# The matmuls of the w_out and down products, regrouped by stationary operand across two PSUM banks

## The chip, the cores and the metric

The kernel runs on one core of a Trainium2 chip. The metric is the device time of one execution in microseconds (us), measured from outside the profile; lower is better. A profiled execution also has a span, which runs from its first to its last recorded instruction and is a little shorter than its device time.

The engines have short names in the profile. PE is TensorE running matmuls, and PEld is TensorE loading a stationary operand. DVE is VectorE, ACT is ScalarE, POOL is GpSimd. SP is the engine that issues most of the transfers.

## The reference

The kernel computes one layer of an encoder on 512 tokens of width 1024, all in float32:

```python
n = rms_norm(h, norm_mix_pre)
proj = n @ w_in                       # gMLP u, v | q, k, v | gates
y_a = gmlp_spatial_gating(gelu(z_gmlp), ...)
y_b = mixture of three dilated window attentions
merged = g_a * (y_a @ w_branch_a) + g_b * (y_b @ w_branch_b)
mix_out = merged @ w_out
h = h + rms_norm(mix_out, norm_mix_post)
n2 = rms_norm(h, norm_mlp_pre)
hid = square(relu(n2 @ w_up))
mlp_out = hid @ w_down
h = h + rms_norm(mlp_out, norm_mlp_post)
```

The change touches two of these products: `merged @ w_out`, in which 1024 values are summed for each output, and `hid @ w_down`, in which 4096 are.

## The kernel before

**A product in three parts.** Each float32 operand is split into a high part and a low part in a reduced format, fp32r: ACT writes `hi`, and DVE writes `lo = raw - hi`. A product of two operands is then three matmuls into one PSUM bank: `mm3` (lines 82 to 86) issues high by high (L84), high by low (L85) and low by high (L86). In the first two the stationary operand, the one held in the array, is the same tile `ah`; in the third it is `al`.

**The two products of the change.** Both are token-major: tokens are the rows of the output. There are four token tiles `t` of 128 tokens, and each has two output halves `hf` of 512 columns. Each half has a PSUM bank of its own, so `all_banks` (line 526) takes all eight banks: `accs[t][hf]`. The stationary operand is the activation (`mh`, `ml` for w_out; `hh`, `hl` for down), a block of 128 features by the 128 tokens of `t`. The moving operand is 512 columns of the weight. So the two halves of one token tile use the same stationary operands.

w_out has 8 blocks `k` of 128 features, down has 32 blocks `f`. For the first 4 blocks of w_out, and the first 28 of down, the order is block by block, and within a block `t`, `hf`, and the three parts. The last four blocks (`KLAST`, `NLAST`) are kept in SBUF and run token tile by token tile: for each `t`, the whole of half 0 (4 blocks by 3 parts, 12 matmuls), then the whole of half 1. So a tile's outputs are finished one after the other while the matmuls of later tiles still run. w_out has 192 matmuls and down 768.

**What follows a token tile.** `post_norm` (line 529) takes a tile's two banks. For each half, ACT squares it and sums the squares (L534), and DVE multiplies it by the gain (`y`, L538). With the second half, DVE finishes the sum of squares (L90 and L93) and POOL raises it to the power -0.5 (L96). DVE then scales and adds the residual (L541, two instructions). After down, the result goes out in two transfers (L659). After w_out there is a second norm (L574 squares, `xn` L578), eight transposes on PE (`pt`, L581), and the split into `n2h` and `n2l` (L79, L80), which the up product reads.

**From w_out to up.** The up product (`pu`) starts with the first two token tiles only: for its first four blocks it does columns 0 to 255 first, and columns 256 to 511 once all four are begun. These short matmuls fill PE while the norms of the last token tiles finish.

**What sets the order.** Each engine runs its instructions in order. The framework places the instructions of each engine by a timeline that it simulates when the kernel is built, so an instruction may stand on its engine at another place than the code has it; the transposes of a token tile stand some microseconds after its norm, among other matmuls.

Of the kernel before, what the change touches and what calls it, by code (L numbers as in the profile page):

```python
# [19 lines left out]
KD = D // P  # L20
FF = 4096
KF = FF // P
# [14 lines left out]
def block_kernel(ctx: ExitStack, tc: tile.TileContext, x, norm_mix_pre, w_in, b_gate, ln_v_gain, ln_v_bias,  # L37
                 w_spatial, b_spatial, w_branch_a, w_branch_b, w_out, norm_mix_post, norm_mlp_pre, w_up,
                 w_down, norm_mlp_post, ident_c, rope_c, mask_c, perm_c, out):
    nc = tc.nc  # L40
# [22 lines left out]
    def wload(shape, srcs, name):  # L63
        raw = wpool.tile([P] + shape, F32, name=name, tag="raw")
        for dst, src in srcs(raw):
            nc.sync.dma_start(dst, src)
        return raw

    def wsplit(raw, pl=None, bufs=None, tag="w", sub=None):
        pl = pl or wpool  # L70
        shape = list(raw.shape)
        hi = pl.tile(shape, F32R, name="hi", tag=tag + "hi", bufs=bufs)
        lo = pl.tile(shape, F32R, name="lo", tag=tag + "lo", bufs=bufs)
        nc.scalar.activation(hi, raw, AF.Copy)  # L74
        (sub or nc.vector).tensor_tensor(lo, raw, hi.bitcast(F32), op=ALU.subtract)  # L75
        return hi, lo

    def split_into(hi, lo, src):
        nc.scalar.activation(hi, src, AF.Copy)  # L79
        nc.vector.tensor_tensor(lo, src, hi.bitcast(F32), op=ALU.subtract)  # L80

    def mm3(ps, a, b, start, stop):
        (ah, al), (bh, bl) = a, b
        nc.tensor.matmul(ps, ah, bh, start=start, stop=False)  # L84
        nc.tensor.matmul(ps, ah, bl, start=False, stop=False)  # L85
        nc.tensor.matmul(ps, al, bh, start=False, stop=stop)  # L86

    def rstd_of(ss, mult, eps=EPS):
        t = small.tile([P, 1], F32, name="rs_in")
        nc.vector.tensor_scalar(t, ss[:, 0:1], mult, eps, op0=ALU.mult, op1=ALU.add)  # L90
        if ss.shape[1] == 2:
            t2 = small.tile([P, 1], F32, name="rs_in2")
            nc.vector.scalar_tensor_tensor(t2, ss[:, 1:2], mult, t, op0=ALU.mult, op1=ALU.add)  # L93
            t = t2
        r = small.tile([P, 1], F32, name="rs_out")
        nc.gpsimd.tensor_tensor(r, t, neghalf[:, :1], op=ALU.pow)  # L96
        return r
# [16 lines left out]
    start = ExitStack()  # L114
# [63 lines left out]
    for i in range(4):  # L178
        if i + 1 < 4:
            norm_x(blocks[i + 1], xts[i + 1])  # L180
        b = blocks[i]
        pv = psA.tile([P, GW], F32, name="pv", tag="acc", bufs=4)
        for k in range(KD):
            sl = slice(b * P, (b + 1) * P)
            mm3(pv, (nh[:, k, sl], nl[:, k, sl]), w0[k], k == 0, k == KD - 1)
        split_into(v0h[:, b], v0l[:, b], pv)
# [32 lines left out]
    def feature_tile(wh, wl, nk, mh, ml, tag="acc"):  # L219
        ps = psA.tile([P, S], F32, name="pf", tag=tag, bufs={"acc": 4, "S": 2}[tag])  # L220
        for k in range(nk):
            mm3(ps, (wh[:, k], wl[:, k]), (mh[:, k], ml[:, k]), k == 0, k == nk - 1)
        return ps
# [237 lines left out]
    for g2 in range(2):  # L461
        raw = wload([KD, 2 * P], lambda r: [(r, fcols(w_in, COL_U + g2 * 2 * P, KD, 2 * P))], "uw")
        for j in range(2):
            g = 2 * g2 + j
            wh, wl = wsplit(raw[:, :, j * P:(j + 1) * P], sub=nc.gpsimd)
            ps = feature_tile(wh, wl, KD, nhn, nln, "S")
# [5 lines left out]
            t = gpool.tile([P, 4, P], F32, name="sv", bufs=2)  # L472
# [10 lines left out]
    mh = mpool.tile([P, KD, S], F32R, name="mh")  # L483
    ml = mpool.tile([P, KD, S], F32R, name="ml")
    gp = ExitStack()
    gapool = pool(gp, "gapool", bufs=2)
    for d2 in range(4):
# [3 lines left out]
        for j in range(2):  # L491
# [3 lines left out]
            for br in range(2):  # L495
                wh, wl = wsplit(raws[br][:, :, sl])
                ps = feature_tile(wh, wl, KD, nhn, nln)
# [26 lines left out]
    halves = [slice(0, 512), slice(512, 1024)]  # L524

    def all_banks():
        return [[psB.tile([P, 512], F32, name="pd", tag=tg, bufs=4) for _ in range(2)] for tg in ("tp", "tp", "acc", "acc")]

    def post_norm(pss, gain, yp, dst, res):
        ss = small.tile([P, 2], F32, name="ss2")  # L530
        ys = []
        for hf, hs in enumerate(halves):
            junk = yp.tile([P, 512], F32, name="junk", bufs=1)
            nc.scalar.activation(junk, pss[hf], AF.Square, accum_out=ss[:, hf:hf + 1])  # L534
            if hf:
                r = rstd_of(ss, 1.0 / D)
            y = yp.tile([P, 512], F32, name="y", bufs=2)
            nc.vector.tensor_tensor(y, pss[hf], gain[:, hs], op=ALU.mult)  # L538
            ys.append(y)
        for hf, hs in enumerate(halves):  # L540
            nc.vector.scalar_tensor_tensor(dst[:, hs], ys[hf], r, res[:, hs], op0=ALU.mult, op1=ALU.add)  # L541
# [3 lines left out]
    wopool = pool(wo, "wopool", bufs=KLAST)  # L545
    accs = all_banks()

    def w_out_mm(t, k, hf, wh, wl):
        ts_ = slice(t * P, (t + 1) * P)
        mm3(accs[t][hf], (mh[:, k, ts_], ml[:, k, ts_]), (wh[:, halves[hf]], wl[:, halves[hf]]), k == 0, k == KD - 1)  # L550

    last = []
    for k0 in range(0, KD, 2):
        raw = wload([2, D], lambda r: [(r, w_out[k0 * P:(k0 + 2) * P].rearrange("(k p) c -> p k c", p=P))], "wow")
        for j in range(2):
            k = k0 + j
            if k < KD - KLAST:
                wh, wl = wsplit(raw[:, j])
                for t in range(4):
                    for hf in range(2):  # L560
                        w_out_mm(t, k, hf, wh, wl)
            else:
                last.append((k, *wsplit(raw[:, j], wopool, tag="wo")))
    ypool = pool(wo, "ypool")
    for t in range(4):
        ts_ = slice(t * P, (t + 1) * P)
        for hf in range(2):
            for k, wh, wl in last:
                w_out_mm(t, k, hf, wh, wl)
        post_norm(accs[t], gain2[:, 0], ypool, h2[:, t], h2[:, t])  # L570
        ss = small.tile([P, 2], F32, name="ss")
        for hf, hs in enumerate(halves):
            junk = ypool.tile([P, 512], F32, name="junk", bufs=1)
            nc.scalar.activation(junk, h2[:, t, hs], AF.Square, accum_out=ss[:, hf:hf + 1])  # L574
        r = rstd_of(ss, 1.0 / D)
        xn = ypool.tile([P, D], F32, name="xn2")
        for q, hs in enumerate(halves):
            nc.vector.scalar_tensor_tensor(xn[:, hs], h2[:, t, hs], r, gain2[:, 1, hs], op0=ALU.mult, op1=ALU.mult)  # L578
            pt = psB.tile([P, 4, P], F32, name="pt2", tag="tp", bufs=4)
            for j in range(4):  # L580
                nc.tensor.transpose(pt[:, j], xn[:, (4 * q + j) * P:(4 * q + j + 1) * P], ident)  # L581
            ks = slice(4 * q, 4 * q + 4)
            split_into(n2h[:, ks, ts_], n2l[:, ks, ts_], pt)
# [24 lines left out]
    for f2 in range(KF // 2):  # L608
        raw = wload([KD, 2 * P], lambda r: [(r, fcols(w_up, f2 * 2 * P, KD, 2 * P))], "upw")
        for j in range(2):  # L610
            f = 2 * f2 + j
            wh, wl = wsplit(raw[:, :, j * P:(j + 1) * P], *((epool, None, "e") if f < NSPLIT - 3 else ()))
            ps = psB.tile([P, S], F32, name="pu", tag="acc", bufs=4)
# [14 lines left out]
    lpool = pool(dn, "lpool", bufs=NLAST)  # L628
    accs = all_banks()

    def down(t, f, hf, hh, hl, wh, wl):
        ts_ = slice(t * P, (t + 1) * P)
        mm3(accs[t][hf], (hh[:, ts_], hl[:, ts_]), (wh[:, halves[hf]], wl[:, halves[hf]]), f == 0, f == KF - 1)

    last = []
    for f2 in range(KF // 2):
        raw = wload([2, D], lambda r: [(r, w_down[f2 * 2 * P:(f2 + 1) * 2 * P].rearrange("(k p) c -> p k c", p=P))], "dnw")
        for j in range(2):
            f = 2 * f2 + j
            end = f >= KF - NLAST  # L640
            wh, wl = wsplit(raw[:, j], *((lpool, 1, "l") if f == KF - NLAST else ()))
            hp = lpool if end else dpool
            hh = hp.tile([P, S], F32R, name="hh")
            hl = hp.tile([P, S], F32R, name="hl")
            split_into(hh, hl, hids[f])
            if end:
                last.append((f, hh, hl, wh, wl))
            else:
                for t in range(4):
                    for hf in range(2):  # L650
                        down(t, f, hf, hh, hl, wh, wl)
    for t in range(4):
        for hf in range(2):
            for f, hh, hl, wh, wl in last:
                down(t, f, hf, hh, hl, wh, wl)
        o = lpool.tile([P, D], F32, name="o", bufs=2)
        post_norm(accs[t], gain2[:, 2], lpool, o, h2[:, t])
        for hs in halves:
            nc.sync.dma_start(out[t * P:(t + 1) * P, hs], o[:, hs])  # L659
# [41 lines left out]
```

## Time and profile before

| | |
|---|---|
| Time, median of 3 runs | 842.24 us (841.08 to 842.56) |
| The profiled execution | 842.03 us, of which its span is 840.2 us |
| PE busy in the span | 826.9 us, 98% |
| Instructions | 9719, of which 3867 matmuls and 3867 loads of a stationary operand |
| w_out's matmuls | from 436.0 to 481.1 us |
| down's matmuls | from 659.8 to 833.7 us |

Matmuls overlap: the profile gives each one a duration of 389 ns, but the next one starts before it ends. What a stream of matmuls costs is read from the distance between their starts. A matmul's row has the line of `mm3` that issued it, its output `pd` and its two operands; the profile sorts the operands by name, so `pd<-hi,hh` is the high part of the weight against the high part of the hidden activation.

### The profile page before, as it was taken

How to read it: one execution, taken by the hardware profiler on the slowest of the kernel's cores; microseconds unless marked ns; L12 is line 12 of the kernel's file. 1: busy time of each engine (PE TensorE's matmuls, PEld its weight loads, DVE VectorE, ACT ScalarE, POOL GpSimd, SP SyncE). 2: the span in 40 equal slices, each digit the busy share in tenths (PEclk: the TensorE clock that was granted, in tenths of full speed). 3: DMA queues.
4: the chain of work that ended last, by engine and by line, in shares of the span. 5: the costliest groups of instructions: out<-in, count | busy, mean ns of one | idle time of the engine just before them, and what ended most of it. 6: DMA issues, size and time to landing. Idle time of an engine off the chain costs nothing. (4 is left out here: it accounts for less than half of the span.)

```text
span 840.2 us, 9719 instructions
## 1 busy us (share of the span) xinstructions
PE 826.9 (98%) x3867; PEld 693.9 (83%) x3867; DVE 419.4 (50%) x711; ACT 293.3 (35%) x479; POOL 74.9 (9%) x67
## 2 busy tenths in 40 slices
PE   7999999999999999999999999999999999999997
PEld 5899888888888778888888898888888888888885
DVE  6422788878874647433334744333333433333425
ACT  6322243435344353333233533222222322333312
POOL 2000123232214200000010100000000000000001
PEclk9999999999999999999999999999999999999999
DMA  9433233323114131431457103333323132222202
GB/s 306 129 101 88 68 96 101 84 67 96 56 52 125 51 100 62 140 101 50 151 195 236 44 2 101 100 101 101 101 100 101 53 131 86 87 98 99 101 1 100
DMA packets 69278, 83.14 MB, mean 99 GB/s; under 512 B 1849, under 2 KB 57297, under 8 KB 69234
## 3 DMA queue, kind: packets, MB, share of 16 engines
q1 hardware_dynamic: 67810, 77.67, 29.3%
q0 software_dynamic: 1424, 4.87, 1.7%
q8 instruction: 30, 0.49, 0.2%
q14 instruction: 14, 0.11, 0.0%
HBM read 80.43 MB, written 2.10 MB: 98 GB/s over the span
## 5 line engine op out<-in xcount | busy, mean ns | idle before, releaser
L84 PE MATMUL pf<-nh,hi 128*128 128x512 f32 x352 | 138.7, 394 | 0.6 <-DVE u L445 0.6
L86 PE MATMUL pf<-nh,lo 128*128 128x512 f32 x352 | 139.3, 396 | 0.0
L85 PE MATMUL pf<-nl,hi 128*128 128x512 f32 x352 | 138.1, 392 | 0.0
L85 PE MATMUL pu<-n2l,hi 128*128 128x512 f32 (+1 forms) x288 | 105.9, 369 | 0.1
L84 PE MATMUL pu<-n2h,hi 128*128 128x512 f32 (+1 forms) x288 | 105.1, 368 | 0.0
L86 PE MATMUL pu<-n2h,lo 128*128 128x512 f32 (+1 forms) x288 | 104.5, 364 | 0.0
L85 PE MATMUL pd<-lo,hh 128*128 128x512 f32 x256 | 99.6, 389 | 0.0
L84 PE MATMUL pd<-hi,hh 128*128 128x512 f32 x256 | 99.3, 389 | 0.0
L86 PE MATMUL pd<-hi,hl 128*128 128x512 f32 x256 | 98.6, 389 | 0.0
L75 DVE TENSOR_TENSOR lo<-upw,hi 128x1024 fp32r<-128x1024 f32 x32 | 39.1, 1225 | 103.0 <-ACT hi L74 103.0
L84 PEld LDWEIGHTS pf<-nh,hi 128*128 128x128 f32 x352 | 66.2, 188 | 14.3 <-DVE u L445 0.9
L86 PEld LDWEIGHTS pf<-nh,lo 128*128 128x128 f32 x352 | 66.2, 188 | 14.3 <-issue 0.2
L85 PEld LDWEIGHTS pf<-nl,hi 128*128 128x128 f32 x352 | 66.2, 188 | 14.1
L74 ACT ACTIVATE hi<-upw 128x1024 fp32r<-128x1024 f32 x32 | 33.8, 1060 | 111.7 <-PE pu L85 100.6
L80 DVE TENSOR_TENSOR hl<-hid,hh 128x512 fp32r<-128x512 f32 x32 | 21.9, 691 | 80.6 <-ACT hh L79 80.6
L84 PEld LDWEIGHTS pu<-n2h,hi 128*128 128x128 f32 x288 | 53.8, 188 | 9.9
L86 PEld LDWEIGHTS pu<-n2h,lo 128*128 128x128 f32 x288 | 54.0, 188 | 9.4
L85 PEld LDWEIGHTS pu<-n2l,hi 128*128 128x128 f32 x288 | 54.1, 188 | 8.6 <-DVE n2l L80 0.3
L247 POOL TENSOR_TENSOR sw<-sw,rope 32x512 f32<-32x512 f32 x24 | 42.4, 1767 | 176.8 <-DVE sw L245 159.6
L84 PEld LDWEIGHTS pd<-hi,hh 128*128 128x128 f32 x256 | 48.0, 188 | 10.1
L85 PEld LDWEIGHTS pd<-lo,hh 128*128 128x128 f32 x256 | 48.0, 188 | 10.1
L86 PEld LDWEIGHTS pd<-hi,hl 128*128 128x128 f32 x256 | 48.0, 188 | 9.8
(201 smaller groups left out, 1306.2 us busy)
## 6 DMA issues: line engine op xcount, KB each, us to landing
upw<-in_w_up_dram SPq DMA_DIRECT2D x16, 1024.0 KB, 5.5
dnw<-in_w_down_dram SPq DMA_DIRECT2D x16, 1024.0 KB, 4.8
qkw<-in_w_in_dram SPq DMA_DIRECT2D x24, 512.0 KB, 4.7
gw<-in_w_in_dram SPq DMA_DIRECT2D x8, 1024.0 KB, 5.3
slab<-in_w_in_dram SPq DMA_DIRECT2D x6, 1024.0 KB, 12.8
wow<-in_w_out_dram SPq DMA_DIRECT2D x4, 1024.0 KB, 4.9
w0raw<-in_w_in_dram SPq DMA_DIRECT2D x4, 512.0 KB, 7.0
uw<-in_w_in_dram SPq DMA_DIRECT2D x2, 1024.0 KB, 5.1
```

Of the source, the lines that this page charges most:

```text
L74: nc.scalar.activation(hi, raw, AF.Copy)
L75: (sub or nc.vector).tensor_tensor(lo, raw, hi.bitcast(F32), op=ALU.subtract)
L80: nc.vector.tensor_tensor(lo, src, hi.bitcast(F32), op=ALU.subtract)
L84: nc.tensor.matmul(ps, ah, bh, start=start, stop=False)
L85: nc.tensor.matmul(ps, ah, bl, start=False, stop=False)
L86: nc.tensor.matmul(ps, al, bh, start=False, stop=stop)
L247: nc.gpsimd.tensor_tensor(sw, sw, rope[:, 1], op=ALU.mult)
```

## The change

`mm3_pair` takes both banks of a token tile. It goes through the same three parts, and issues each part for half 0 and then for half 1. So the stationary operand changes twice in six matmuls instead of three or four times, and every matmul writes the other bank of the pair than the one before it. The loops over `hf` go. In the last four blocks of each product the two halves of a token tile now run side by side through the four blocks. Number, shapes and operands of the matmuls stay as they are, and so does everything that follows them.

```diff
+    def mm3_pair(banks, a, bs, start, stop):
+        ah, al = a
+        bhs, bls = zip(*bs)
+        for lhs, rhs, first, last in ((ah, bhs, start, False), (ah, bls, False, False), (al, bhs, False, stop)):
+            for ps, r in zip(banks, rhs):
+                nc.tensor.matmul(ps, lhs, r, start=first, stop=last)
...
-    def w_out_mm(t, k, hf, wh, wl):
+    def w_out_mm(t, k, wh, wl):
         ts_ = slice(t * P, (t + 1) * P)
-        mm3(accs[t][hf], (mh[:, k, ts_], ml[:, k, ts_]), (wh[:, halves[hf]], wl[:, halves[hf]]), k == 0, k == KD - 1)
+        mm3_pair(accs[t], (mh[:, k, ts_], ml[:, k, ts_]), [(wh[:, hs], wl[:, hs]) for hs in halves], k == 0, k == KD - 1)
...
                 for t in range(4):
-                    for hf in range(2):
-                        w_out_mm(t, k, hf, wh, wl)
+                    w_out_mm(t, k, wh, wl)
...
-        for hf in range(2):
-            for k, wh, wl in last:
-                w_out_mm(t, k, hf, wh, wl)
+        for k, wh, wl in last:
+            w_out_mm(t, k, wh, wl)
...
-    def down(t, f, hf, hh, hl, wh, wl):
+    def down(t, f, hh, hl, wh, wl):
         ts_ = slice(t * P, (t + 1) * P)
-        mm3(accs[t][hf], (hh[:, ts_], hl[:, ts_]), (wh[:, halves[hf]], wl[:, halves[hf]]), f == 0, f == KF - 1)
+        mm3_pair(accs[t], (hh[:, ts_], hl[:, ts_]), [(wh[:, hs], wl[:, hs]) for hs in halves], f == 0, f == KF - 1)
...
                 for t in range(4):
-                    for hf in range(2):
-                        down(t, f, hf, hh, hl, wh, wl)
+                    down(t, f, hh, hl, wh, wl)
     for t in range(4):
-        for hf in range(2):
-            for f, hh, hl, wh, wl in last:
-                down(t, f, hf, hh, hl, wh, wl)
+        for f, hh, hl, wh, wl in last:
+            down(t, f, hh, hl, wh, wl)
```

## Rows read from the trace of the kernel before

**Rows 1.** From the profile's page: busy time, share of the span and number of instructions of each engine.

```profile
PE 826.9 (98%) x3867; PEld 693.9 (83%) x3867; DVE 419.4 (50%) x711; ACT 293.3 (35%) x479; POOL 74.9 (9%) x67
```

**Rows 2.** Busy time in three stages: w_out, the start of up, and down. Columns: the stretch in us, its length, busy us (instructions) of each engine, granted clock, share of the transfer engines, GB/s.

```profile
core 0: us, PE busy (x) PEld busy (x) DVE busy (x) ACT busy (x) POOL busy (x), PEclk, DMA share, GB/s
435.90:480.50 44.60, 44.60 (x205) 37.02 (x205) 25.88 (x41) 19.07 (x37) 2.76 (x5) 1.00 0.53 175
480.50:500.00 19.50, 19.42 (x163) 19.10 (x162) 9.81 (x20) 6.47 (x16) 1.65 (x3) 1.00 0.01 2
...
659.00:834.00 175.00, 175.00 (x773) 144.63 (x771) 67.15 (x81) 52.76 (x75) 1.65 (x3) 1.00 0.25 86
```

**Rows 3.** The instructions that write or read the banks `pd`, by line: count, duration in ns (least, median, most), starts of the first and the last in us. The rows with `hh` and `hl` are down's, those with `mh` w_out's.

```profile
L84 PE MATMUL pd<-hi,hh x256: 389/389/391, 659.8 to 833.2; 128*128 128x512 f32 x128
L85 PEld LDWEIGHTS pd<-lo,hh x256: 187/188/188, 659.8 to 833.3; 128*128 128x128 f32 x128
L86 PE MATMUL pd<-hi,hl x256: 388/389/393, 660.3 to 833.7; 128*128 128x512 f32 x128
L84 PE MATMUL pd<-hi,mh x64: 389/389/474, 436.0 to 480.5; 128*128 128x512 f32 x64
```

**Rows 4.** PE in order of time within down: start, duration, engine, line, instruction. A bank is left after each L86.

```profile
754.82 0.39 PE L86 MATMUL pd<-hi,hl 128*128 128x512 f32 x1
755.05 0.39 PE L84 MATMUL pd<-hi,hh 128*128 128x512 f32 x1
755.27 0.39 PE L85 MATMUL pd<-lo,hh 128*128 128x512 f32 x1
755.50 0.39 PE L86 MATMUL pd<-hi,hl 128*128 128x512 f32 x1
```

**Rows 5.** PE in order of time within up, where 24 matmuls in a row write one bank (first and tenth of ten).

```profile
525.93 0.39 PE L84 MATMUL pu<-n2h,hi 128*128 128x512 f32 x1
...
528.00 0.39 PE L84 MATMUL pu<-n2h,hi 128*128 128x512 f32 x1
```

**Rows 6.** PE in order of time in a stretch of the q and k projections (first and tenth of ten).

```profile
161.22 0.40 PE L84 MATMUL pf<-nh,hi 128*128 128x512 f32 x1
...
163.32 0.40 PE L84 MATMUL pf<-nh,hi 128*128 128x512 f32 x1
```

**Rows 7.** The end of the kernel in order of time, all engines (PE's rows thinned out). In brackets: idle time of the engine before, and what ended it.

```profile
830.98 0.39 PE L86 MATMUL pd<-hi,hl 128*128 128x512 f32 x1
...
831.47 0.60 ACT L534 ACTIVATE junk<-pd 128x512 f32<-128x512 f32 x1 [2.03 <-PE pd L86]
...
832.19 0.69 DVE L538 TENSOR_TENSOR y<-pd,gain 128x512 f32<-128x512 f32 x1 [0.41 <-ACT junk L534]
...
832.80 0.14 DVE L90 TENSOR_SCALAR rs_in<-ss 128x1 f32<-128x1 f32 x1
...
833.47 0.39 PE L85 MATMUL pd<-lo,hh 128*128 128x512 f32 x1
...
833.70 0.39 PE L86 MATMUL pd<-hi,hl 128*128 128x512 f32 x1
834.19 0.60 ACT L534 ACTIVATE junk<-pd 128x512 f32<-128x512 f32 x1 [2.03 <-PE pd L86]
...
834.91 0.16 DVE L93 SCALAR_TENSOR_TENSOR rs_in<-ss,rs_in 128x1 f32<-128x1 f32 x1 [1.97 <-ACT junk L534]
```

**Rows 8.** ACT in order of time where w_out goes over into up: two squares with sums one right after the other, and ACT's next instruction right after such a sum.

```profile
479.03 0.63 ACT L574 ACTIVATE junk<-h 128x512 f32<-128x512 f32 x1 [3.10 <-DVE h L541]
...
479.78 0.63 ACT L574 ACTIVATE junk<-h 128x512 f32<-128x512 f32 x1
...
480.41 0.58 ACT L79 ACTIVATE n2h<-pt 128x512 fp32r<-128x512 f32 x1
480.89 0.59 ACT L534 ACTIVATE junk<-pd 128x512 f32<-128x512 f32 x1
...
481.46 0.59 ACT L79 ACTIVATE n2h<-pt 128x512 fp32r<-128x512 f32 x1
```

**Rows 9.** DVE in order of time in the same stretch.

```profile
481.02 0.69 DVE L80 TENSOR_TENSOR n2l<-pt,n2h 128x512 fp32r<-128x512 f32 x1 [0.33 <-ACT n2h L79]
...
488.22 0.14 DVE L90 TENSOR_SCALAR rs_in<-ss 128x1 f32<-128x1 f32 x1
488.47 0.16 DVE L93 SCALAR_TENSOR_TENSOR rs_in<-ss,rs_in 128x1 f32<-128x1 f32 x1
489.36 1.42 DVE L578 SCALAR_TENSOR_TENSOR xn<-h,rs_out,gain 128x512 f32<-128x512 f32 x2 [0.73 <-POOL rs_out L96]
```

**Rows 10.** PE in order of time: the first four transposes of the last token tile after w_out.

```profile
492.77 0.60 PE L581 MATMUL pt<-ident,xn 128*128 128x128 f32 x4
```

**Rows 11.** Who waited for whom from 435 to 500 us (us in total, times, longest): the one row in which TensorE waits.

```profile
PEld pu L85 <- DVE n2l L80: 0.3, 1, 0.3
```

**Rows 12.** Groups by line: the two instructions that clear a bank of up (count, busy us, mean ns, idle before).

```profile
L605 DVE TENSOR_TENSOR hid<-pu,relu 128x512 f32<-128x512 f32 x32 | 21.9, 683 | 4.5 <-ACT relu L604 4.5
...
L604 ACT ACTIVATE relu<-pu 128x512 f32<-128x512 f32 x32 | 18.6, 583 | 4.6 <-PE pu L86 4.6
```

**Rows 13.** PE near the start of the kernel.

```profile
11.21 0.63 PE L86 MATMUL pv<-hi,nl 128*128 128x512 f32 x1
11.64 0.63 PE L84 MATMUL pv<-hi,nh 128*128 128x512 f32 x1
```

## The prediction

> **What bounds the kernel now.** I began with busy time by engine, to see whether any engine but PE can matter: PE is busy for 98% of the span, DVE for 50%, ACT for 35% [rows 1]. Next the stages: in w_out and in down PE has no idle time at all, in the 19.50 us between w_out and the steady part of up it is idle for 0.08, and the granted clock is 1.00 in all three, the upper of its two levels [rows 2]. So the two products cost what their stream of matmuls costs, and DVE, ACT and the transfers have slack. Since a matmul's 389 ns overlap the next one, the third view is the tile view of the banks, from which a pace comes. Down's L86 row has 256 matmuls from 660.3 to 833.7 us: 173.4 / 255 = 0.680 us for a group of three, 226.7 ns a matmul [rows 3]. The reader is to see that this is more than the columns alone take: 512 columns at the upper level, 2.4 GHz, are 213.3 ns. The other 13.4 ns are all that a better order could win, 960 x 13.4 = 12.8 us over w_out's 192 and down's 768 matmuls. Then PE in order of time within down shows whether those 13.4 ns hang on the two things that the change alters. Last come the rows at the kernel's end, the only stretch without cover by PE.
>
> **The body of the two products: 0.** The change keeps all 960 matmuls and alters who follows whom. Before, two of three follow a matmul in the same bank (L84 to L85, L85 to L86) and one follows a matmul in another (L86 to L84). In order of time the three distances are 0.23, 0.22 and 0.23 us, and the first of these is the change of bank [rows 4]. So a change of bank is neither cheaper nor dearer than staying, within the 0.01 us of the rows. As to the stationary operand, L85 has the same `ah` as L84 before it, and yet there is one load for each L85, 188 ns long like the others [rows 3], and L84 to L85 takes the 0.22 us of the rest [rows 4]. The load is issued for every matmul and nothing is saved where it repeats. Both things that become more frequent already occur, at 226.7 ns, and I take that for all 960.
>
> The Trainium skill says on its page "TensorE: Matmul & The Clock Gate", Part 2, first step, that load and compute are separate instructions so that one load can serve many matmuls. The trace disagrees for this data type: 3867 loads stand beside 3867 matmuls [rows 1]. What it would be worth here is the second rival.
>
> Bounds: the trace has other paces for the same shape. Up runs at 2.07 / 9 = 230 ns [rows 5], and a stretch of the projections at 2.10 / 9 = 233.3 ns [rows 6]. Nothing in the names of their operands tells why, so the new order might fall into one of them: +0.003 x 960 = +3.2 us or +0.0067 x 960 = +6.4 us. Below, the bound is the 12.8 us above. I take 0, since the nearest rows are those of the same operands.
>
> **The end of the kernel: +0.6 us.** The last token tile now completes both halves together, so the post-norm of half 0 loses its cover. Before, half 0's last matmul starts at 830.98 and its square at 831.47, 0.49 later; half 1's at 833.70 and its square at 834.19, also 0.49 later [rows 7]. After, the last matmul of half 0 is the last but one of the kernel, at 833.47, so its square starts at 833.96. The second square can't start at 834.19, since ACT is at work: two squares with sums in a row stand 0.75 us apart (479.03 to 479.78) [rows 8], which gives 834.71, 0.52 late. L93 follows a square by 834.91 - 834.19 = 0.72 [rows 7], so it comes at 835.43. On DVE, half 0's `y` starts 0.72 after its square (831.47 to 832.19), at 834.68; L90 follows 0.61 after that, at 835.29 [rows 7]; L93 follows L90 by 0.25 [rows 9], at 835.54. The later of the two is 835.54, 0.63 after the 834.91 of before, and everything behind it (POOL's power, the scaling, the transfers) is a chain that shifts with it. I take 0.6. From below: ACT can begin another instruction 0.57 after a square (480.89 to 481.46) [rows 8], which makes the second square 834.53, 0.34 late. From above: if DVE does the second `y` before L93, another 0.61 is added, 1.2.
>
> The three earlier tiles of down have the same delay, but 24 matmuls of the next tile, 5.4 us, hide it. The last tile finds DVE free.
>
> **From w_out to up: +0.3 us.** The same delay of 0.6 falls on each token tile's norm after w_out. Most of it is covered: the last tile's `xn` is done at 489.36 + 1.42 = 490.78 [rows 9] and its transposes stand at 492.77 [rows 10], 2.0 us later. One place has no cover. PE's first matmuls of up already wait 0.3 us for `n2l` [rows 11], written by DVE from 481.02 on [rows 9], behind ACT's `n2h` at 480.41, which queues behind the squares of another tile's norm at 479.03 and 479.78 [rows 8]. If that norm is 0.6 late, so is this wait, unless the framework places `n2h` ahead of the squares. I take half, 0.3. From below: the wait of 0.3 goes, -0.3. From above: 0.6 here and another 0.7 if the new placing puts transposes badly, 1.3.
>
> **Edits at nothing.** The second bank of token tile 3 is first written by the 20th matmul of down instead of the 22nd. Up's last bank is cleared by 0.58 + 0.68 us of ACT and DVE [rows 12] after the last matmul of up, which starts just before 659.8 us; the 20th starts 19 x 0.227 = 4.3 us after 659.8 [rows 3], so 3 us are left. Buffers: `hl` is last read by the 24th matmul of a block as before, `hh` by the 22nd instead of the 23rd, so splits for later blocks start no later. Transfers, POOL and SP see the same instructions. There are no new waits between engines.
>
> **Sum.** 842.03 + 0 + 0.6 + 0.3 = 842.9 for the profiled execution. That one lies 0.21 below the median of 842.24, so the forecast is 842.24 + 0.9 = 843.1 us. Its own range, with the ends of the two small terms (0.34 - 0.3 and 1.2 + 1.3), is 842.3 to 844.7.
>
> **Rivals.**
>
> First, alternating banks speeds the stream up. It would do so if part of the 13.4 ns were a wait of one accumulation for the one before it in the same bank. For it: up, with 24 in a row in one bank, runs at 230 ns, slower than down's 226.7 [rows 3, 5]. Against it: within down the change of bank is no quicker than the two steps without one [rows 4]. Half of the 13.4 ns gone would be 960 x 6.7 = 6.4 us, 836.7; all of it 830.3. 17%.
>
> Second, the repeated stationary operand costs no exchange. Before, one matmul in three has the operand of its predecessor, after, four in six: 320 more matmuls without the exchange, 320 x 13.4 = 4.3 us, 838.8. Against it: L85 has such a predecessor and shows neither a missing load nor a shorter distance [rows 3, 4]. 3%.
>
> Third, on the other side: the stream locks into a slower pace. Its place is the body of down; its price is that of up's pace, 3.2 us (846.3), or of the projections', 6.4 us (849.5) [rows 5, 6]. For it: the operations there are the same as down's, so the pace hangs on something finer, and the order of reads is such a thing. Against it: all of down's 768 matmuls keep one pace over token tiles, weights and buffers [rows 3]. It decides from the point where the sum passes 842.24 + 1.68: (1.68 - 0.9) / 960 = 0.8 ns a matmul. 13%.
>
> Fourth, the clock falls. Near the start two matmuls of this shape stand 0.43 us apart [rows 13], 512 columns at the lower level, 1.2 GHz; if a tenth of the 960 ran like that, it would be +96 x 0.20 = 19 us, 862. Against it: down already goes through eight banks in every block, and the granted clock is 1.00 [rows 2]. 1%. The same page of the Trainium skill, "A second HAM failure mode: psum-queue depth-cycling", tells of a kernel that went through PSUM banks in every iteration and whose clock fell and rose again; the trace disagrees so far.
>
> Fifth, the new order doesn't reach the time: the framework places the norms so that neither term is seen, 842.2 (-0.3 to +0.3). 7%.
>
> **How the numbers follow.** The forecast's own case has the remaining 59%. What a measurement of this kernel can tell from no change is about 0.2%, 1.68 us: 840.6 to 843.9. Of the 59%, 51 lie within that and 8 above. Faster: the first rival without its smallest gains (16) and the second (3), 19%. Slower: 8 + 13 + 1 = 22%. The same: 51 + 7 + 1 = 59%. The range goes down to 838.5, which takes in the second rival and half of the first, and up to 846.0, which takes in the smaller part of the third; it leaves out about 9 below and 9 above.
>
> **What would show it.** The tile view of the banks: L84, L85 and L86 become the one line of `mm3_pair` with 3 x 256 and 3 x 64 matmuls; the pace between their starts, 226.7 ns, decides between the forecast and the first three rivals. Loads must stay as many as matmuls. At the end, the first square should start about 0.5 us after the last matmul but one, the second 0.75 after the first, and L93 1.8 us after the start of the last matmul instead of 1.2. The waits from 435 to 500 us should show TensorE waiting 0.3 to 0.9 us for `n2l`. The prediction is wrong if the pace leaves 226.7 by more than 1 ns, or if the end shifts by more than 1.2 us.

## The result, and the profile after

The changed kernel takes 844.82 us (median of 9 runs, 843.06 to 845.57), the kernel before 842.24 us (9 runs beside them): +2.58 us, a ratio of 1.0029 with a 95% interval of 1.0019 to 1.0039. It is slower, inside the range given (838.5 to 846.0), though by more than the forecast of +0.9 us. By the bands of the prediction, which put 59% on 840.6 to 843.9 and 22% on slower, the less likely of the two came. In the profiled execution the span is 843.3 us.

The stages of the changed kernel, the same stretches as in [rows 2]:

```profile
core 0: us, PE busy (x) PEld busy (x) DVE busy (x) ACT busy (x) POOL busy (x), PEclk, DMA share, GB/s
435.90:480.50 44.60, 44.60 (x203) 36.99 (x202) 24.26 (x38) 17.39 (x32) 2.45 (x5) 1.00 0.54 179
480.50:500.00 19.50, 18.78 (x152) 17.78 (x151) 11.29 (x22) 7.07 (x18) 1.94 (x4) 1.00 0.00 1
...
659.00:834.00 175.00, 175.00 (x773) 144.88 (x773) 65.65 (x79) 52.06 (x73) 1.64 (x3) 1.00 0.24 85
```

PE is still never idle in w_out and down, at the same granted clock. Between w_out and up it now idles for 0.72 us (19.50 - 18.78) where it idled for 0.08.

The tile view of the banks, which answers to [rows 3] (all three parts have the line of `mm3_pair` now):

```profile
L93 PEld LDWEIGHTS pd<-hi,hh x256: 187/188/188, 661.6 to 834.6; 128*128 128x128 f32 x128
L93 PE MATMUL pd<-hi,hh x256: 389/389/398, 661.8 to 834.8; 128*128 128x512 f32 x128
L93 PEld LDWEIGHTS pd<-lo,hh x256: 187/188/188, 662.0 to 835.0; 128*128 128x128 f32 x128
L93 PE MATMUL pd<-lo,hh x256: 389/389/397, 662.3 to 835.2; 128*128 128x512 f32 x128
L93 PEld LDWEIGHTS pd<-hi,hl x256: 187/188/188, 662.5 to 835.5; 128*128 128x128 f32 x128
L93 PE MATMUL pd<-hi,hl x256: 387/389/393, 662.7 to 835.7; 128*128 128x512 f32 x128
```

The last row runs from the fifth to the last of down's 768 matmuls, 763 distances in 173.0 us: 226.7 ns each, as before. Each matmul still has its load of 188 ns, also where four in a row have the same stationary operand (the two rows of loads with `hh`).

The end of the kernel, which answers to [rows 7] (a matmul row with x2 stands for one in each bank):

```profile
835.46 0.61 PE L93 MATMUL pd<-hi,hl 128*128 128x512 f32 x2
835.95 0.60 ACT L541 ACTIVATE junk<-pd 128x512 f32<-128x512 f32 x1 [4.03 <-PE pd L93]
836.44 0.20 ACT L541 ACTIVATION_READ_ACCUMULATOR junk<-pd 128x1 f32 x1
836.67 0.60 ACT L541 ACTIVATE junk<-pd 128x512 f32<-128x512 f32 x1
836.67 0.69 DVE L545 TENSOR_TENSOR y<-pd,gain 128x512 f32<-128x512 f32 x1 [1.82 <-ACT junk L541]
...
837.28 0.14 DVE L97 TENSOR_SCALAR rs_in<-ss 128x1 f32<-128x1 f32 x1
837.39 0.69 DVE L545 TENSOR_TENSOR y<-pd,gain 128x512 f32<-128x512 f32 x1
838.00 0.15 DVE L100 SCALAR_TENSOR_TENSOR rs_in<-ss,rs_in 128x1 f32<-128x1 f32 x1
```

L541, L545, L97 and L100 are the L534, L538, L90 and L93 of before. The last matmul starts at 835.46 + 0.23 = 835.69. The last step of the sum of squares (L100) starts at 838.00, 2.31 us later; before it was 834.91 - 833.70 = 1.21. And DVE does the second `y` ahead of it.

From w_out to up, PE in order of time:

```profile
480.48 0.62 PE L93 MATMUL pd<-hi,ml 128*128 128x512 f32 x2
480.94 1.04 PE L586 MATMUL pt<-ident,xn 128*128 128x128 f32 x8
482.22 0.51 PE L84 MATMUL pu<-n2h,hi 128*128 128x256 f32 x2 [0.25 <-ACT n2h L79]
482.95 0.39 PE L85 MATMUL pu<-n2l,hi 128*128 128x256 f32 x1 [0.22 <-DVE n2l L80]
...
494.89 0.28 PE L86 MATMUL pu<-n2h,lo 128*128 128x256 f32 x1
495.01 1.03 PE L586 MATMUL pt<-ident,xn 128*128 128x128 f32 x8
496.30 0.51 PE L84 MATMUL pu<-n2h,hi 128*128 128x256 f32 x2 [0.25 <-ACT n2h L79]
```

The second token tile's transposes (480.94) stand behind the last matmul of w_out, so nothing is left for PE while ACT and DVE split them. The last tile's (495.01) stand behind all 96 short matmuls on columns 0 to 255, with the same effect; before, they began at 492.77 [rows 10], behind 87 of the 96, and the others filled PE. The waits from 435 to 508 us, where [rows 11] was the only one:

```profile
PEld pu L84 <- ACT n2h L79: 1.0, 2, 0.5
...
PEld pu L85 <- DVE n2l L80: 0.6, 2, 0.4
```

### The profile page after: what moved, and what is told of

It is laid out like the page before. It is cut to its first block, busy times and chain, and to the rows that moved or that the text cites. A ratio compares the mean times of both kernels' runs of the same rounds, so it can differ in the third digit from the quotient of the medians.

```text
span 843.3 us, 9716 instructions
## 1 busy us (share of the span) xinstructions
PE 828.1 (98%) x3867; PEld 694.4 (82%) x3867; DVE 418.9 (50%) x711; ACT 292.5 (35%) x479; POOL 74.3 (9%) x67
## 4 chain that ended last, share of the span: by engine, by line
PE 93%; DVE 3%; ACT 2%; issue 1%; DMA 1%; POOL 0%; SPq 0%; DVEq 0%; POOLq 0%; ACTq 0%
PE pd L93 24%; PE pf L86 11%; PE pf L85 11%; PE pf L84 11%; PE pu L84 7%; PE pu L86 7%; PE pu L85 7%; PE pv L84 4%; PE pv L85 4%; PE pv L86 4%; PE py L413 1%; PE psb L313 1%; DMA w0raw<-in_w_in_dram 1%; ACT hi L74 0%; PE pt L384 0%
## 5 line engine op out<-in xcount | busy, mean ns | idle before, releaser
L86 PE MATMUL pf<-nh,lo 128*128 128x512 f32 x352 | 139.4, 396 | 0.0
L86 PE MATMUL pu<-n2h,lo 128*128 128x512 f32 (+1 forms) x288 | 105.6, 367 | 0.0
L93 PE MATMUL pd<-lo,hh 128*128 128x512 f32 x256 | 78.9, 389 | 0.0
L93 PE MATMUL pd<-hi,hh 128*128 128x512 f32 x256 | 78.9, 389 | 0.0
L93 PE MATMUL pd<-hi,hl 128*128 128x512 f32 x256 | 78.4, 389 | 0.0
L86 PEld LDWEIGHTS pf<-nh,lo 128*128 128x128 f32 x352 | 66.2, 188 | 13.6 <-issue 0.2
L86 PEld LDWEIGHTS pu<-n2h,lo 128*128 128x128 f32 x288 | 54.1, 188 | 9.8
L93 PEld LDWEIGHTS pd<-lo,hh 128*128 128x128 f32 x256 | 48.1, 188 | 10.1
L93 PEld LDWEIGHTS pd<-hi,hl 128*128 128x128 f32 x256 | 48.1, 188 | 9.9
L93 PEld LDWEIGHTS pd<-hi,hh 128*128 128x128 f32 x256 | 48.1, 188 | 9.9
```

Of the source, the lines that this page charges most:

```text
L93: nc.tensor.matmul(ps, lhs, r, start=first, stop=last)
```

## The experiments

Two stretches are compared in all of them, because the start of w_out differs from profile to profile (435.2 to 437.6 us in the ten kernels) with nothing changed ahead of it. The transition is the time from the first matmul of w_out to the first matmul of up with 512 columns. The end is the time from the start of the last matmul to the end of the span. Both come from one profile of each kernel. The bounds of the transition, in the kernel before:

```profile
435.95 0.40 PE L84 MATMUL pd<-hi,mh 128*128 128x512 f32 x1
...
506.02 0.39 PE L84 MATMUL pu<-n2h,hi 128*128 128x512 f32 x1
```

and in the changed kernel:

```profile
436.49 0.63 PE L93 MATMUL pd<-hi,mh 128*128 128x512 f32 x2
...
507.96 0.40 PE L84 MATMUL pu<-n2h,hi 128*128 128x512 f32 x1
```

Below the row of the change, times are medians of 11 or 12 runs, beside 33 or 35 of the kernel before on the same chip: 842.29 us for the first four, 842.18 for the others. The ratio and its interval are taken over the runs as a whole, so the ratio can differ a little from the quotient of the two medians, 1.0015 for w_out alone.

| Kernel | us over before | Ratio, 95% interval | Transition | End |
|---|---|---|---|---|
| before | | | 70.07 | 6.54 |
| the change | +2.58 | 1.0029 [1.0019, 1.0039] | 71.47 | 7.63 |
| w_out alone | +1.28 | 1.0010 [1.0000, 1.0020] | 71.07 | 6.55 |
| down alone | +1.02 | 1.0009 [1.0000, 1.0017] | 70.05 | 7.64 |
| all but the last four blocks | +0.01 | 1.0000 [0.9991, 1.0009] | 70.05 | 6.54 |
| the last four blocks alone | +2.43 | 1.0024 [1.0016, 1.0033] | 71.50 | 7.64 |
| the change, sum before `y` | +1.19 | 1.0015 [1.0007, 1.0024] | 70.59 | 7.18 |
| the change, last block by halves | +1.85 | 1.0021 [1.0012, 1.0030] | 71.16 | 7.17 |
| the change, last two by halves | +0.65 | 1.0008 [0.9999, 1.0017] | 70.61 | 6.53 |
| before, with up in two banks | +0.13 | 0.9999 [0.9990, 1.0008] | 70.04 | 6.54 |

In every row the two stretches together give the difference in time to within 0.3 us, for the change 1.40 + 1.09 = 2.49 of 2.58. So no other part of the kernel has to be looked for.

**The theory and its rival.** The theory: the loss lies where the two halves of a token tile finish together, 1.1 us at the end and 1.4 in the transition, and the order of the other matmuls costs nothing. The rival: the new order as such slows the stream, in proportion to the matmuls that have it. The first four kernels put the new order into one part each; their edits are shown against the changed kernel.

w_out alone (down's functions and loops are those of the kernel before):

```diff
-        for f, hh, hl, wh, wl in last:
-            down(t, f, hh, hl, wh, wl)
+        for hf in range(2):
+            for f, hh, hl, wh, wl in last:
+                down(t, f, hf, hh, hl, wh, wl)
```

> w_out in the new order, down in the old one. If the loss comes where the two halves of a token tile finish together, this kernel has the part between w_out and up and not the part at the end: 1.4 us over the kernel before, with 71.5 us from the first matmul of w_out to the first 512-column matmul of up (70.1 before) and 6.5 us from the start of the last matmul to the end of the span. If the new order slows the stream of matmuls, the loss goes by their number, 192 of 960: 0.5 us of the 2.5.

Measured: +1.28 us, transition 71.07, end 6.55. The part in the transition came alone. The time by itself would allow the rival's 0.5 us too (the interval reaches from 0 to 1.7 us). In the profile the transition is 0.4 us shorter than in the changed kernel, though PE, ACT and DVE have the same rows in the same order there and TensorE's loads wait as long (1.0 us for `n2h`, 0.6 for `n2l`). The difference lies behind the last wait, in up's short matmuls. In this kernel:

```profile
496.39 0.28 PE L86 MATMUL pu<-n2h,lo 128*128 128x256 f32 x1
...
506.59 0.28 PE L86 MATMUL pu<-n2h,lo 128*128 128x256 f32 x1
```

and the same two in the changed kernel:

```profile
497.24 0.28 PE L86 MATMUL pu<-n2h,lo 128*128 128x256 f32 x1
...
507.84 0.28 PE L86 MATMUL pu<-n2h,lo 128*128 128x256 f32 x1
```

Between them lie 90 distances, of 113.3 ns here and 117.8 ns there, at a granted clock of 1.00 in both. The kernel before has 117.8 as well. What makes the 4.5 ns was not found.

down alone (w_out's are those of before):

```diff
-        for k, wh, wl in last:
-            w_out_mm(t, k, wh, wl)
+        for hf in range(2):
+            for k, wh, wl in last:
+                w_out_mm(t, k, hf, wh, wl)
```

> down in the new order, w_out in the old one. If the loss comes where the halves finish together: 1.1 us over the kernel before, all of it after the start of the last matmul (7.6 us to the end of the span, 6.5 before), and 226.7 ns a matmul in down. If the stream is slowed: 768 of 960 matmuls, 2.0 us over the kernel before.

Measured: +1.02 us, all of it at the end, 7.64. The rival wanted 2.0 us here, which is above the interval (0.0017 of 842.29 is 1.4 us).

The new order everywhere but in the last four blocks:

```diff
-        for k, wh, wl in last:
-            w_out_mm(t, k, wh, wl)
+        for hf in range(2):
+            for k, wh, wl in last:
+                w_out_half(t, k, hf, wh, wl)
...
-        for f, hh, hl, wh, wl in last:
-            down(t, f, hh, hl, wh, wl)
+        for hf in range(2):
+            for f, hh, hl, wh, wl in last:
+                down_half(t, f, hf, hh, hl, wh, wl)
```

Here `w_out_half` and `down_half` are `w_out_mm` and `down` of the kernel before.

> The new order in the first 4 blocks of w_out and the first 28 of down (768 of the 960 matmuls), the last four blocks of each as before, half by half. If the loss comes from the finish alone: the time of the kernel before, within 0.5 us, with the transition at 70.1 and the end at 6.5 us. If the body has a share: slower by up to 4/5 of the loss, 2.0 us.

Measured: +0.01 us, both stretches those of before. 768 matmuls in the new order neither win nor lose more than the interval allows, 0.8 us.

The last four blocks alone:

```diff
                 for t in range(4):
-                    w_out_mm(t, k, wh, wl)
+                    for hf in range(2):
+                        w_out_half(t, k, hf, wh, wl)
...
                 for t in range(4):
-                    down(t, f, hh, hl, wh, wl)
+                    for hf in range(2):
+                        down_half(t, f, hf, hh, hl, wh, wl)
```

> The opposite: the bodies as before, only the last four blocks in the new order (192 of the 960 matmuls). If the loss comes from the finish: all of it, 2.5 us over the kernel before, transition 71.5 and end 7.6 us. If it goes by the number of reordered matmuls: 0.5 us.

Measured: +2.43 us, transition 71.50, end 7.64: the whole loss with a fifth of the reordered matmuls. The rival is out.

**Why the end cost 1.1 and not 0.6.** The next kernel is the changed one with the second `y` forced behind the sum on DVE:

```diff
-            nc.vector.scalar_tensor_tensor(t2, ss[:, 1:2], mult, t, op0=ALU.mult, op1=ALU.add)
+            summed.append(nc.vector.scalar_tensor_tensor(t2, ss[:, 1:2], mult, t, op0=ALU.mult, op1=ALU.add))
...
-            nc.vector.tensor_tensor(y, pss[hf], gain[:, hs], op=ALU.mult)
+            if hf:
+                with tc.issue_after(getattr(summed[-1], "ins", summed[-1])):
+                    nc.vector.tensor_tensor(y, pss[hf], gain[:, hs], op=ALU.mult)
+            else:
+                nc.vector.tensor_tensor(y, pss[hf], gain[:, hs], op=ALU.mult)
```

> The changed kernel with one order fixed: on DVE the second `y` is issued behind the last step of the sum of squares (L93 before). By the prediction's sum for that order, the end is 0.6 us over the kernel before instead of 1.1: 7.1 to 7.2 us from the start of the last matmul. If the order of these two is not what made the end dearer than forecast, it stays at 7.6. Between w_out and up each norm loses 0.6 us of its delay; if the delay of the norms sets the waits there, the transition falls from 71.5 towards 70.8; if the new places of the transposes do, it stays at 71.5. Time: 0.6 to 2.0 us over the kernel before.

Measured: +1.19 us, end 7.18, transition 70.59. Its end in order of time (L102 is L93 of before):

```profile
835.69 0.61 PE L93 MATMUL pd<-hi,hl 128*128 128x512 f32 x2
836.17 0.60 ACT L543 ACTIVATE junk<-pd 128x512 f32<-128x512 f32 x1 [4.03 <-PE pd L93]
...
836.89 0.60 ACT L543 ACTIVATE junk<-pd 128x512 f32<-128x512 f32 x1
...
837.76 0.16 DVE L102 SCALAR_TENSOR_TENSOR rs_in<-ss,rs_in 128x1 f32<-128x1 f32 x1
837.83 0.69 DVE L549 TENSOR_TENSOR y<-pd,gain 128x512 f32<-128x512 f32 x1
```

The last step of the sum starts at 837.76, 1.84 us after the start of the last matmul (835.69 + 0.23), the value that the prediction worked out. So of the 1.1 us, 0.64 is the lost cover (7.18 - 6.54) and 0.45 the place of the second `y` (7.63 - 7.18). In the transition 0.9 of the 1.4 us goes too. What is left there shows on ACT:

```profile
482.00 0.63 ACT L585 ACTIVATE junk<-h 128x512 f32<-128x512 f32 x1 [3.68 <-DVE h L554]
482.54 0.19 ACT L585 ACTIVATION_READ_ACCUMULATOR junk<-h 128x1 f32 x1
482.63 0.58 ACT L79 ACTIVATE n2h<-pt 128x512 fp32r<-128x512 f32 x1
```

PE began these transposes at 481.41, but `n2h` stands on ACT behind a square of the next tile's norm, which starts at 482.00, when that tile's `h` is there. The first matmul of up waits until 483.26.

**How far apart the finishes have to be.** In two kernels the last block, or the last two, go half by half again (`n` is 1 or 2; the change itself has 0, the kernel before 4):

```diff
-        for f, hh, hl, wh, wl in last:
+        for f, hh, hl, wh, wl in last[:4 - n]:
             down(t, f, hh, hl, wh, wl)
+        for hf in range(2):
+            for f, hh, hl, wh, wl in last[4 - n:]:
+                down_half(t, f, hf, hh, hl, wh, wl)
```

The same is done in w_out. One block by halves:

> The changed kernel with the very last block of w_out and of down half by half, so that half 0 is done 0.68 us before half 1 (0.23 in the changed kernel, 2.72 before). If the distance between the two finishes sets the cost, this lies between: the end at 7.2 us (the second `y` still stands before the sum), the transition between 70.1 and 71.5; 0.6 to 1.9 us over the kernel before. If any pairing in the last blocks costs, whatever the distance, the full 2.5 us.

Measured: +1.85 us, transition 71.16, end 7.17. Both stretches lie between, and the end is the 7.2 that was worked out.

Two blocks by halves:

> The changed kernel with the last two blocks half by half: half 0 is done 1.36 us before half 1, which is more than one square with its sum and its `y` (0.72 + 0.61) take. By the theory of the finish the end is that of the kernel before, 6.5 us, and the transition is near 70.1 us: 0 to 0.4 us over the kernel before, with 864 of 960 matmuls in the new order. By any cost that goes with the number of paired matmuls: 2 us and more.

Measured: +0.65 us, end 6.53, transition 70.61. The end is that of the kernel before with 1.36 us between the finishes; the transition keeps 0.5 us, which I had not expected; TensorE's loads still wait 0.8 us for `n2h` and `n2l` there, against 0.3 before. Its interval (0.9999 to 1.0017) holds no change as well as 1.4 us. The end in order of time:

```profile
833.83 0.60 ACT L541 ACTIVATE junk<-pd 128x512 f32<-128x512 f32 x1 [3.39 <-PE pd L86]
...
834.71 0.39 PE L86 MATMUL pd<-hi,hl 128*128 128x512 f32 x1
835.16 0.14 DVE L97 TENSOR_SCALAR rs_in<-ss 128x1 f32<-128x1 f32 x1
835.19 0.60 ACT L541 ACTIVATE junk<-pd 128x512 f32<-128x512 f32 x1 [0.67 <-PE pd L86]
...
835.91 0.16 DVE L100 SCALAR_TENSOR_TENSOR rs_in<-ss,rs_in 128x1 f32<-128x1 f32 x1 [0.61 <-ACT junk L541]
```

The second square waits for PE again, not for ACT, and the last step of the sum starts 835.91 - 834.71 = 1.20 us after the start of the last matmul, as before.

**Whether a bank sets the pace at all.** The first rival had one argument: up, with 24 matmuls in a row in one bank, is slower than down. This kernel is the one before with up's later blocks two at a time, alternating between two banks:

```diff
+    def up_pair(pss, ws):
+        for k in range(KD):
+            for a, b, first, last_ in ((0, n2h, k == 0, False), (0, n2l, False, False), (1, n2h, False, k == KD - 1)):
+                for ps, w in zip(pss, ws):
+                    nc.tensor.matmul(ps, w[a][:, k], b[:, k], start=first, stop=last_)
...
+        if 2 * f2 >= NSPLIT:
...
+            up_pair(pss, ws)
```

> The kernel before, but up's 28 later blocks go two at a time, matmul by matmul between two banks (stationary operands differ there). Up's pace was 228.9 ns with 24 matmuls in a row in one bank, down's 226.7. If the bank sets the pace, up falls to 226.7 or below: 672 x 2.2 ns = 1.5 us less than the kernel before, more if alternation as such is quicker. If the bank doesn't matter: 228.9 ns, and the time of the kernel before or up to 1 us more, since two blocks are evacuated together at the end of up.

Measured: +0.13 us, within the noise. The tile view of up's banks:

```profile
L612 PE MATMUL pu<-n2h,hi x224: 388/392/394, 506.7 to 659.4; 128*128 128x512 f32 x112
...
L612 PE MATMUL pu<-n2h,lo x224: 388/392/395, 507.2 to 660.3; 128*128 128x512 f32 x112
```

From the first matmul (506.7) to the last (660.3) there are 671 distances in 153.6 us: 228.9 ns. In the kernel before, the same stretch runs from 506.02 to the last start in this row, 659.6, also 153.6 us:

```profile
L86 PE MATMUL pu<-n2h,lo x288: 278/388/388, 482.0 to 659.6; 128*128 128x512 f32 x112, 128*128 128x256 f32 x32
```

The bank is not what makes up slower than down.

No kernel here beats the one before; the best with the new order is the one that gives back the order of the last four blocks, and it is equal.

## Why the prediction was right and where it was off

**The body at 0: right.** Down's pace is 226.7 ns in the changed kernel as before, and the kernel with the new order in the bodies alone is at +0.01 us. The two things that the order makes more frequent were both to be seen in the old trace, at the old price [rows 3, 4]. One of its bounds was too wide: up's 230 ns came from ten rows, and over all of up's 672 long matmuls the pace is 228.9, which makes the third rival's lower price 960 x 2.2 ns = 2.1 us instead of 3.2.

**The first rival fell** by that kernel and by up in two banks. **The second fell** by the changed kernel's own trace: six matmuls need two changes of the stationary operand where they needed four, yet four matmuls in a row with one stationary operand keep four loads of 188 ns and the pace of 226.7. The Trainium skill's page "TensorE: Matmul & The Clock Gate", Part 2, first step, says that weights can be loaded once for many matmuls; no run here shows that. The 3867 loads beside 3867 matmuls, in which the prediction saw a disagreement, show what this program issues. What it would gain without the repeated loads stays open, since no kernel here leaves one out. **The third and fourth** did not come: the pace is the same and the granted clock is 1.00 in down. PE was never idle there, so this says nothing of changing banks with idle time in between. **The fifth** did not come either; the two small terms were real.

**The end, +0.6: the mechanism right, the term mis-sized.** It measured 1.1. The step that failed is the choice between the two orders on DVE: I took the old one, with L93 ahead of the second `y`, and kept the other for the bound ("if DVE does the second `y` before L93, another 0.61 is added, 1.2"). The framework chose the other: 837.39 stands ahead of 838.00. The old trace held both orders: at the kernel's end L93 came first, but in the last token tile of w_out the second `y` did:

```profile
484.21 0.68 DVE L538 TENSOR_TENSOR y<-pd,gain 128x512 f32<-128x512 f32 x1
484.81 0.15 DVE L93 SCALAR_TENSOR_TENSOR rs_in<-ss,rs_in 128x1 f32<-128x1 f32 x1
```

With L93 forced ahead of the second `y`, the last step of the sum starts 1.84 us after the start of the last matmul, as worked out.

**The transition, +0.3: the mechanism right, the term mis-sized.** It measured 1.4, just above the upper bound of 1.3, and it falls on two places. The first matmul of up that reads `n2l` started before at

```profile
481.77 0.39 PE L85 MATMUL pu<-n2l,hi 128*128 128x256 f32 x1
```

which is 45.82 us after w_out's first matmul. Now it starts at 482.95, 46.46 us after it: 0.64 later. That is the wait at the start of up, where I took half; it came in full, and the second tile's transposes had moved behind the last matmul of w_out. The other 0.76 comes behind the last tile's transposes, the 0.7 that the upper bound had set aside for badly placed ones. Of the waits, the 0.6 us for `n2l` lie within the forecast's 0.3 to 0.9; the 1.0 us for `n2h` were not in it.

The step that failed is "The same delay of 0.6 falls on each token tile's norm". Counted from w_out's first matmul, the `xn` of the four tiles start 0.5, 1.5, 3.1 and 2.3 us later than before. The norms queue behind each other on DVE: before, the first `y` of the second tile still stood ahead of the first tile's `xn`,

```profile
468.15 0.69 DVE L538 TENSOR_TENSOR y<-pd,gain 128x512 f32<-128x512 f32 x1 [0.56 <-ACT junk L534]
...
468.82 1.41 DVE L578 SCALAR_TENSOR_TENSOR xn<-h,rs_out,gain 128x512 f32<-128x512 f32 x2
```

and now it stands behind it, as in the third tile:

```profile
469.86 1.42 DVE L583 SCALAR_TENSOR_TENSOR xn<-h,rs_out,gain 128x512 f32<-128x512 f32 x2 [0.73 <-POOL rs_out L103]
471.20 0.68 DVE L545 TENSOR_TENSOR y<-pd,gain 128x512 f32<-128x512 f32 x1
```

Besides, the first three tiles now have their second `y` ahead of the sum, which only the last had before. The last tile's `xn`:

```profile
492.21 1.41 DVE L583 SCALAR_TENSOR_TENSOR xn<-h,rs_out,gain 128x512 f32<-128x512 f32 x2 [0.73 <-POOL rs_out L103]
```

That is 492.21 - 436.49 = 55.72 us after w_out's first matmul; before it was 489.36 - 435.95 = 53.41 [rows 9]. 2.3 us late is more than the 2.0 us of cover that I had counted on, and the last transposes stand behind the short matmuls. Which of the two, the late norms or the framework's new places, is the cause by itself stays open: when the norms come earlier, the framework places the transposes elsewhere too. In the change, the kernels with one and with two blocks by halves and the one with the sum first, the third tile's `xn` is 3.1, 2.0, 1.5 and 1.6 us late, and the transition is 1.4, 1.1, 0.5 and 0.5 us longer.

**The sum.** With the terms as measured, 842.24 + 0 + 1.1 + 1.4 = 844.7 us, against 844.82. The prediction had both places and the body; its 0.9 was too small because both terms came out near the upper bounds that it had worked out itself (1.1 of 1.2, and 1.4 against 1.3). That the time lies in the range is in part luck: the forecast's own case ended at 844.7, and the range went up to 846.0 for the sake of the third rival, which did not come.

## What to carry to other kernels

An order of matmuls is worth what the pace between their starts gains, and here the old trace held that pace already, since both kinds of neighbour occur in it. What the new order changed is when results are complete: where a product ends and a norm follows, results finished one after the other hid the norm's first half, and 1.4 us between them was enough at the end of this kernel. When such a cover goes, work out both orders on the engines behind it (the framework took the dearer one here), and follow the delays of stages that queue behind each other tile by tile instead of counting one.

## What was not expected of the hardware

The same shape of matmul has a pace of 226.7 ns in down and 228.9 in up, at the same granted clock of 1.00, and the order of banks doesn't move either: down keeps 226.7 with a new bank at every matmul or at every third, up keeps 228.9 with one bank for 24 matmuls or two in turn. What makes the 2.2 ns was not found. Nor does the order settle the pace of up's short matmuls: 117.8 ns in the profile of the changed kernel and 113.3 in that of w_out alone, in one and the same order.

The granted clock is not enough to tell how fast matmuls follow each other. The prediction took the 0.43 us between two matmuls near the kernel's start for the lower level [rows 13], but the granted clock reads 1.00 for that stretch too. The two don't agree, and no run here tells why; the reading of down's body above rests on its pace.

```profile
0.00:12.00 12.00, 7.53 (x16) 4.17 (x17) 5.95 (x14) 6.86 (x15) 2.14 (x7) 1.00 0.84 294
```
